# V of four heads with x as the stationary operand, and SiLU gates in pairs of their own

## The chip, the core and the metric

The kernel runs on one core of a Trainium2 chip. The metric is the device time of one execution in microseconds (us). TensorE (PE) multiplies a stationary operand of 128 x 128, which a separate weight load brings in (PEld in the profile), with a streamed (moving) operand of up to 512 columns, into accumulators in PSUM. VectorE (DVE) and ScalarE (ACT) do elementwise work and read PSUM; GpSimd (POOL) and SyncE (SP) here issue transfers. Every product is made from float32 values split in a high and a low part (float32r): high x high + high x low + low x high.

## The reference

One layer over 512 tokens of width 2048, with three token mixers (A: forgetting attention, B: chunked attention, C: stick-breaking attention) of four heads of width 128:

```python
hn = rmsnorm(x, norm_g)
proj = jnp.einsum('bsd,dc->bsc', hn, w_in)
br = proj[..., :QKVG_COLS].reshape(b, s, N_BRANCH, 4, BRANCH_W)      # q, k, v and a gate path for each branch
gates = jax.nn.sigmoid(proj[..., QKVG_COLS + N_HEADS:] + b_gate).reshape(b, s, N_BRANCH, D_MODEL)
...
yc = stick_breaking_attention(to_heads(br[:, :, 2, 0]), to_heads(br[:, :, 2, 1]), to_heads(br[:, :, 2, 2]))
ys = jnp.stack([from_heads(ya), from_heads(yb), from_heads(yc)], axis=2)
ys = ys * jax.nn.silu(br[:, :, :, 3])
up = jnp.einsum('bsnw,nwd->bsnd', ys, w_up)
merged = jnp.sum(gates * up, axis=2)
return x + jnp.einsum('bsd,de->bse', merged, w_out)
```

The change touches V (`br[:, :, n, 2]`), the gate path G (`br[:, :, n, 3]`) and the order of the projection's columns. What is computed stays the same.

## The kernel before, in words

**Layout.** Activations are kept transposed: features on the 128 partitions, the 512 tokens along the free axis. x (times `norm_g`, not yet normalised) lies in SBUF as 16 tiles of 128 features, each as `Parts` with high and low values of two token halves of 256 (`x1`, `x2`, and combinations `t23`, `t4`). A projected column block of 128 (Q, K, V or G of one head, or a 128-wide slice of the merge gates) is one column.

**Pairs.** Two columns are made together by `PairTask` (line 593) with seven products in place of eight (Strassen's scheme in Winograd's form, over two columns, two halves of the 2048 features and two token halves). Each product is a `Pair` unit (line 572) of eight k-steps: the weight block is stationary, x streams. For each k-step there is a 512-wide matmul (`high`, line 667: weight's high part against x's high and low) and a 256-wide one (`low`, line 682: weight's low part against x's high). `stream` (line 1541) goes through the list `units`; a unit may begin with its low step (`low_first`) when the one before ended with its own. Products accumulate onto earlier ones where they can (`onto`), so that the seven use few PSUM banks (`accs`); the other four banks (`atts`) serve attention. `sums` (line 630) makes two of the seven weights on DVE from loaded ones; two are added by POOL's accumulating loads (`add_up`). After a product, `after_of` (line 697) copies or adds it out of PSUM.

**Weights.** SP loads a weight block of 512 KB into one of six `raw` tiles (`NR`). `prep` (line 385) then splits it: ACT copies the high part into `wh` (line 247), DVE subtracts to get `wl` (line 251). There are three buffers of each, and a unit is prepared two units ahead (`LA`).

**Order.** `Flow` plans at build time: generators yield what they wait for and what an engine's next piece costs and when it is due, and the program order of PE, ACT and DVE is written out in the order of that plan. Tiles of 128 x 512 come from a pool of 20 (`t2s`, `NT`). SP's and POOL's queues hold transfers; an instruction there that waits holds up those behind it.

**Units.** The first group (`first_quad`, line 1198, nine units) makes Q, K, V and G of head C0 by direct products, with four banks, while x arrives. Then comes a pair of merge-gate columns; then for each head of C, B and A a pair Q+K, a pair of merge gates, a pair V+G, and a pair of merge gates. Merge-gate columns are normalised and stored to HBM until the up projection. Attention stages (`schedule`, line 1276) are spawned at set units after a head's pairs and mix with the stream on PE.

**V and G of a head.** V comes out with its 128 features on partitions, but the product with the attention weights needs it with tokens on partitions. `v_trans` (line 1087) does four PE transposes into one `att` bank, then four ACT copies (line 1102) and four DVE operations (line 1105) that scale each token by its norm and split into high and low. `silu` (line 1110) normalises G (`by_norm`, line 514), and makes SiLU from it. `av` (line 1133) multiplies V with the attention weights and the result with SiLU.

**After the projections** come the up projection with merge gates (32 units) and the output projection (eight pairs).

Of the kernel before, what the change touches and what calls it, by code (L numbers as in the profile page):

```python
# [15 lines left out]
P = 128  # L16
HP = P // 2
S = 512
# [135 lines left out]
def act_us(n, x=1):  # L154
    return x * (0.075 + 0.00095 * n)
# [7 lines left out]
def hybrid_kernel(  # L163
# [5 lines left out]
    consts: bass.AP,  # L169
    w_one: bass.AP,  # L170
    w_two: bass.AP,
    w_col: bass.AP,
    rel: bass.AP,
    w_up: bass.AP,
# [17 lines left out]
    def nm(s):  # L192
        uid[0] += 1
        return f"{s}_{uid[0]}"
# [16 lines left out]
    def att():  # L211
        return pt.tile([P, S], F32, tag="att", name=nm("att"))
# [4 lines left out]
    def blk(i):  # L217
        return slice(i * P, (i + 1) * P)
# [135 lines left out]
    class Unit:  # L354


        def __init__(self, mms, after=None, shape=(UK, P), srcs=()):
            self.shape, self.mms, self.after, self.srcs = list(shape), mms, after, srcs
            self.ready_hi, self.ready, self.there, self.raw = Event(), Event(), Event(), None
            self.low_first = False  # L360

        def source_there(self):
            return self.there
# [8 lines left out]
        return wp.tile([P] + list(shape), F32, tag="raw", name=nm("raw"), bufs=NR)  # L372

    def load_unit(u):
        if isinstance(u, Pair):
            if u is u.task.units[0]:
                yield from u.task.load()
            return
        for s in u.srcs:
            yield raws, 1  # L380
            t = raw_tile(u.shape)
            u.raw = t
            u.there.t = fetch(t, s, flow.ready, 4 * u.shape[0] * P * P // 1024, nc.scalar if u is units[0] else nc.sync).t

    def prep(u):
        n = u.shape[0] * P
        u.hi = wp.tile([P] + u.shape, F32R, tag="wh", name=nm("wh"), bufs=LA + 1)
        u.lo = wp.tile([P] + u.shape, F32R, tag="wl", name=nm("wl"), bufs=LA + 1)
        yield u.source_there()
        if u is units[0]:  # L390
            for h in range(2):
                yield ACT, act_us(n // 2)
                nc.scalar.activation(u.hi[:, 2 * h:2 * h + 2, :], u.source()[:, 2 * h:2 * h + 2, :], AF.Copy)
                if h == 0:
                    set_(u.ready_hi)
            yield DVE, dve_us(n)
            nc.vector.tensor_sub(u.lo, u.source(), f(u.hi))
            set_(u.ready)
        else:
            yield from split(u.hi, u.lo, u.source(), n, u.ready, hi_ev=u.ready_hi)  # L400
        u.split_done()
# [170 lines left out]
    class Pair(Unit):  # L572


        def __init__(self, task, i):
            super().__init__(task.mms_of(i), task.after_of(i))
            self.task, self.p = task, task.order[i]
            self.single = task.late or task.plain_end and self.p == 4
            self.onto = None if task.late else {6: 1, 7: 6, 4: 7, 3: 5}.get(self.p)

        def source_there(self):
            if self is self.task.units[0]:
# [10 lines left out]
    class PairTask:  # L593
# [9 lines left out]
        def __init__(self, src1, src2, ops, c1_done=None, c2r_done=None, c2_done=None, late=False, rest=None,  # L603
                     x1_first=False, plain_end=False):
            self.plain_end = plain_end
            self.src, self.ops, self.late, self.rest = (*src1, *src2), ops, late, rest
            self.done = {"c1": c1_done, "c2r": c2r_done, "c2": c2_done}
            self.order = (1, 5, 2, 3, 6, 7, 4) if late else (1, 2, 6, 5, 7, 3, 4)
            if x1_first:
                self.order = (1, 5, 6, 2, 7, 3, 4)  # L610
            self.w, self.there, self.ps = {}, {p: Event() for p in range(1, 8)}, {}
            self.ev = {p: Event() for p in range(1, 8)}
            self.r, self.r_ev, self.c2_ev = None, Event(), Event()
            self.units = [Pair(self, i) for i in range(7)]

        def unit(self, p):
# [34 lines left out]
        def mms_of(self, i):  # L651
            p = self.order[i]
            bank = (0, 1, 2, 0, 0, 1, 2)[i] if self.late else {2: 1, 5: 2, 3: 2}.get(p, 0)
            self.bank = getattr(self, "bank", {})
            self.bank[p] = bank

            def go(u):
# [39 lines left out]
        def after_of(self, i):  # L697
# [68 lines left out]
            def go():  # L766
                if i == 0 and self.rest is not None:
                    spawn(self.rest(self), 1.0)
                if self.late:
                    yield from late()  # L770
                    return
                ps, bank = self.ps[p], accs[self.bank[p]]
                if p == 1:
                    yield from new("u")
                    yield a
# [61 lines left out]
            return go  # L837


    gl = {}  # L840
    yd = {}
    f_ev, f2_ev = Event(), Event()
    fd, fd2 = dp.tile([NQ * NH, S], F32, name="fd"), dp.tile([NH, S], F32, name="fd2")

# [41 lines left out]
    class Head:  # L886
# [197 lines left out]
            nc.scalar.activation(z, z, AF.Exp)  # L1084
            set_(self.event("s", i))

        def v_trans(self):
            yield self.event(V)
            for j in range(3):
                yield self.event("hl", j)  # L1090
            yield atts, 1
            yield PE, 0.44
            ps = att()
            for b in range(QB):
                nc.tensor.transpose(ps[:, blk(b)], self.c[V][:, blk(b)], identf)  # L1095
            give(t2s)
            yield t2s, 2
            self.v = h, lo = pair_of("v")
            yield rstd_ev
            yield ACT, 4 * act_us(P)  # L1100
            for b in range(QB):
                nc.scalar.activation(h[:, blk(b)], ps[:, blk(b)], AF.Copy, scale=rcol[:, b:b + 1])
            yield DVE, 4 * dve_us(P)
            for b in range(QB):
                nc.vector.scalar_tensor_tensor(lo[:, blk(b)], ps[:, blk(b)], rcol[:, b:b + 1], f(h[:, blk(b)]),
                                               op0=ALU.mult, op1=ALU.subtract)
            set_(self.event("v"))
            give(atts)
# [48 lines left out]
        def stages(self):  # L1157
# [12 lines left out]
            return g, [(v, self.v_trans), (o - 3, self.silu), (o, self.av)]  # L1170


    def col(n, r, h):
# [13 lines left out]
    def gate_units(late=False, x1_first=False):  # L1187
        n, d = gates.pop(0)

        def keep(i):  # L1190
            def go(c):
# [3 lines left out]
        units.extend(PairTask(gate_col(n, d), gate_col(n, d + 1), ops, keep(0), None, keep(1), late,  # L1195
                              x1_first=x1_first).units)

    def first_quad(head):

        ps, pools = {}, {Q: accs[1], K: accs[2], V: atts, G: atts}  # L1200
        def mms(i):
            def go(u):
# [20 lines left out]
        def take(r):  # L1223
            yield t2s, 1
            c = t2("c")
            if r in (Q, V):
                yield ACT, act_us(S)
                nc.scalar.activation(c, ps[r], AF.Copy)
            else:
                yield DVE, dve_us(S)  # L1230
                nc.vector.tensor_copy(c, ps[r])
            give(pools[r])
            head.c[r] = c
            set_(head.event(r))

# [40 lines left out]
    def schedule(head, a, b):  # L1276
        for (d, g), base in [(g, a) for g in head.stages()[0]] + [(g, b) for g in head.stages()[1]]:
            at(base + d, g, 3.0 if head.last else 5.0)

    def first_head(n, h):  # L1280
        hd = Head(n, h)
        units.extend(first_quad(hd))
        at(OFF["fb"], forget_bias)
        gate_units()
        schedule(hd, OFF["a0"], OFF["b0"])

    def head(n, h, last=False):
# [3 lines left out]
        if not last:  # L1291
            gate_units()
        units.extend(PairTask(col(n, V, h), col(n, G, h), ops, hd.got(V), None, hd.got(G)).units)
        gate_units()
        if last:
            gate_units()
            gate_units(x1_first=True)
        schedule(hd, u0 + 7, u0 + 21)
        return hd

    first_head(C, 0)
    for n, h in [(C, 1), (C, 2), (C, 3)] + [(n, h) for n in (B, A) for h in range(NH)]:
        last_head = head(n, h, (n, h) == (A, NH - 1))


    ys = [None] * 12
# [234 lines left out]
    def stream():  # L1541
        ends_low = False
        for i, u in enumerate(units):
# [7 lines left out]
            if isinstance(u, Pair) and not u.single:  # L1551
# [90 lines left out]
```

## Time and profile before

| | us |
|---|---|
| median of three runs | 1313.18 (1313.05 to 1313.41) |
| the profiled execution | 1313.15 |
| its span, first to last instruction | 1311.4 |
| PE busy in it | 1306.7 |
| DVE busy | 1154.3 |
| ACT busy | 817.8 |
| transfers | 266 MB, mean 203 GB/s |

The granted TensorE clock is 1.0 throughout. A row of the page's groups reads: line of the kernel, engine, operation, tile written <- tiles read, partitions x elements, count | busy us, mean ns of one | idle time of the engine just before, and what ended most of it. A matmul's mean is a latency, as matmuls overlap; its pace is seen from the starts of successive ones. A row of the timeline has start and length in us, engine, line, operation, tiles and count. A row of waits has who waited for whom, the total, the number of waits and the longest, in us. A row of the stretches has its length and then each engine's busy time with its instructions (PE, PEld, DVE, ACT, POOL), the granted clock, the share of the DMA engines and GB/s. A row of transfers has tiles, queue, count, KB of each and median us from issue to landing.

### The profile page before, as it was taken

How to read it: one execution, taken by the hardware profiler on the slowest of the kernel's cores; microseconds unless marked ns; L12 is line 12 of the kernel's file. 1: busy time of each engine (PE TensorE's matmuls, PEld its weight loads, DVE VectorE, ACT ScalarE, POOL GpSimd, SP SyncE). 2: the span in 40 equal slices, each digit the busy share in tenths (PEclk: the TensorE clock that was granted, in tenths of full speed). 3: DMA queues.
4: the chain of work that ended last, by engine and by line, in shares of the span. 5: the costliest groups of instructions: out<-in, count | busy, mean ns of one | idle time of the engine just before them, and what ended most of it. 6: DMA issues, size and time to landing. Idle time of an engine off the chain costs nothing.

```text
span 1311.4 us, 20146 instructions
## 1 busy us (share of the span) xinstructions
PE 1306.7 (100%) x7405; PEld 1143.5 (87%) x7405; DVE 1154.3 (88%) x1723; ACT 817.8 (62%) x1298; POOL 94.8 (7%) x120
## 2 busy tenths in 40 slices
PE   9999999999999999999999999999999999999998
PEld 6888888888888888888888888888888888898887
DVE  8999979788898989988899989899899888897786
ACT  8767657575557665666657665676657655454443
POOL 0010100000010100100100000101000000001000
PEclk9999999999999999999999999999999999999999
DMA  9777676777776777767767777777778855668883
GB/s 344 223 192 190 182 207 170 213 186 194 194 203 190 192 200 187 214 180 194 203 175 221 191 184 201 198 193 187 197 178 277 280 193 168 204 172 254 241 253 95
DMA packets 89794, 266.22 MB, mean 203 GB/s; under 512 B 10704, under 2 KB 12752, under 8 KB 89696
## 3 DMA queue, kind: packets, MB, share of 16 engines
q1 hardware_dynamic: 70400, 203.80, 46.3%
q0 software_dynamic: 15552, 56.63, 25.5%
q10 hardware_dynamic: 3744, 4.52, 1.0%
q8 instruction: 58, 0.95, 0.3%
q14 instruction: 40, 0.33, 0.1%
HBM read 245.21 MB, written 19.70 MB: 202 GB/s over the span
## 4 chain that ended last, share of the span: by engine, by line
PE 99%; DVE 0%; ACT 0%; issue 0%; POOL 0%; ACTq 0%; POOLq 0%
PE acc L266 85%; PE att L266 8%; PE att L1030 1%; PE att L262 1%; PE att L1144 1%; PE att L263 1%; PE att L1145 1%; PE att L261 1%; PE att L1143 1%; PE att L1095 0%; PE att L1245 0%; PE att L1563 0%; PE att L928 0%; DVE m L251 0%; ACT wh L247 0%; DVE wl L251 0%
## 5 line engine op out<-in xcount | busy, mean ns | idle before, releaser
L251 DVE TENSOR_TENSOR wl<-raw,wh 128x1024 fp32r<-128x1024 f32 (+2 forms) x418 | 500.0, 1198 | 103.9 <-ACT wh L247 102.8
L247 ACT ACTIVATE wh<-raw 128x1024 fp32r<-128x1024 f32 (+2 forms) x418 | 434.1, 1039 | 142.2 <-PE acc L266 72.5
L266 PE MATMUL acc<-x,wh 128*128 128x512 f32 x1536 | 394.1, 392 | 0.0
L266 PEld LDWEIGHTS acc<-x,wh 128*128 128x128 f32 x1536 | 281.8, 188 | 56.1 <-issue 2.2
L266 PE MATMUL acc<-t,wh 128*128 128x512 f32 x1104 | 278.9, 393 | 0.0
L266 PEld LDWEIGHTS acc<-t,wh 128*128 128x128 f32 x1104 | 198.5, 189 | 35.3
L266 PEld LDWEIGHTS acc<-x,wl 128*128 128x128 f32 x1504 | 207.8, 190 | 17.1 <-DVE x L450 0.8
L266 PE MATMUL acc<-x,wl 128*128 128x256 f32 (+1 forms) x1504 | 218.9, 285 | 0.0
L266 PE MATMUL acc<-t,wl 128*128 128x256 f32 x1104 | 157.0, 283 | 0.0
L266 PEld LDWEIGHTS acc<-t,wl 128*128 128x128 f32 x1104 | 144.9, 191 | 2.6
L284 POOL DMA_DIRECT2D raw<-in_w_col x92 | 79.5, 864 | 911.1 <-DMA raw<-in_w_col 482.1
L266 PE MATMUL acc<-m,wh 128*128 128x512 f32 (+1 forms) x512 | 109.6, 364 | 0.3 <-DVE m L251 0.3
L266 PEld LDWEIGHTS acc<-m,wh 128*128 128x128 f32 x512 | 86.2, 189 | 13.9 <-DVE m L251 0.5
L797 ACT ACTIVATE u<-acc 128x512 f32<-128x512 f32 x52 | 30.9, 595 | 77.6 <-PE acc L266 75.9
L776 ACT ACTIVATE u<-acc 128x512 f32<-128x512 f32 x53 | 31.8, 599 | 67.8 <-PE acc L266 64.6
L830 ACT ACTIVATE c<-acc 128x256 f32<-128x256 f32 x52 | 19.9, 383 | 83.1 <-PE acc L266 77.6
L642 DVE TENSOR_TENSOR raw<-raw,raw 128x1024 f32<-128x1024 f32 x54 | 65.9, 1221 | 0.5
L636 DVE TENSOR_TENSOR raw<-raw,raw 128x1024 f32<-128x1024 f32 x54 | 65.9, 1220 | 0.3
L266 PE MATMUL att<-y,wh 128*128 128x512 f32 x256 | 65.8, 389 | 0.0
L266 PEld LDWEIGHTS acc<-m,wl 128*128 128x128 f32 x448 | 58.2, 191 | 2.4
L266 PE MATMUL acc<-m,wl 128*128 128x256 f32 x448 | 59.8, 283 | 0.0
L266 PEld LDWEIGHTS att<-y,wh 128*128 128x128 f32 x256 | 48.0, 188 | 10.0
(202 smaller groups left out, 1401.7 us busy)
## 6 DMA issues: line engine op xcount, KB each, us to landing
raw<-in_w_col SPq DMA_DIRECT2D x230, 512.0 KB, 4.3
raw<-in_w_col POOLq DMA_DIRECT2D x92, 512.0 KB, 6.5
raw<-in_w_out SPq DMA_DIRECT2D x40, 512.0 KB, 4.7
gl<-c SPq DMA_DIRECT2D x48, 256.0 KB, 3.0
raw<-in_w_up SPq DMA_DIRECT2D x32, 384.0 KB, 3.2
sg<-gl SPq DMA_DIRECT2D x48, 256.0 KB, 4.3
raw<-in_w_out POOLq DMA_DIRECT2D x16, 512.0 KB, 7.5
xn<-in_xn SPq DMA_DIRECT2D x16, 256.0 KB, 3.3
```

The lines of the kernel that those rows point to most:

```text
L247: nc.scalar.activation(hi, src, AF.Copy)
L251: nc.vector.tensor_sub(lo, src, f(hi))
L261: nc.tensor.matmul(ps, lh, rh, start=start, stop=False, skip_group_check=more)
L262: nc.tensor.matmul(ps, lh, rl, start=False, stop=False, skip_group_check=more)
L263: nc.tensor.matmul(ps, ll, rh, start=False, stop=stop, skip_group_check=more)
L266: nc.tensor.matmul(ps, w, x, start=start, stop=stop, skip_group_check=more)
L284: nc.gpsimd.dma_start(to, src, accum_op=ALU.add)
L636: nc.vector.tensor_add(w[1], w[1], w[5])
L642: nc.vector.tensor_add(w[2], w[2], w[1])
L776: nc.scalar.activation(self.u, ps, AF.Copy)
L797: nc.scalar.activation(self.s, ps, AF.Copy)
L830: nc.scalar.activation(c, ps[:, RH], AF.Copy, scale=-1.0)
```

## The change

- **V.** A `ValueTask` makes V of a branch's four heads (512 columns) at once by the same seven products: x's block of 128 features by 128 tokens is stationary, the weights stream (high and low parts of 256 columns side by side). It has 14 units: each product's eight k-steps are cut in two halves of four, and each half serves two blocks of tokens (`subs`, two `PairTask`s that only supply the steps after the products). The result has tokens on partitions; ACT scales it by each token's norm, SP stores it to HBM, and `value` reads a head's part back and splits it. The transposes are gone. The second block of tokens uses one `att` bank and banks of `accs[0]`.
- **G.** Gates are made in pairs of two heads; the second head's is normalised, stored to HBM and read back in `silu` (`far`, `gd`). In the first group G of head C1 takes the place of V.
- **Order.** `HEADS` lists what follows each head's Q+K pair: s a pair of gates G, g a pair of merge gates, v the next branch's V task. C's V task comes right after the first group. The offset `b0` goes from 20 to 23.
- **Weights.** High and low parts share one tile (`u.w`), in all units. The weights of V's product 7 are loaded, for each half, into two tiles of the `t2s` pool in place of a `raw` tile.

```diff
     def prep(u):
-        n = u.shape[0] * P
-        u.hi = wp.tile([P] + u.shape, F32R, tag="wh", name=nm("wh"), bufs=LA + 1)
-        u.lo = wp.tile([P] + u.shape, F32R, tag="wl", name=nm("wl"), bufs=LA + 1)
+        n = u.shape[0] * u.shape[1]
+        u.w = wp.tile([P, 2] + u.shape, F32R, tag="w", name=nm("w"), bufs=LA + 1)
+        u.hi, u.lo = u.w[:, 0], u.w[:, 1]
...
+        elif isinstance(u.source(), list):
+            h = u.shape[0] // 2
+            for i, t in enumerate(u.source()):
+                ks, evs = slice(i * h, (i + 1) * h), (u.ready, u.ready_hi) if i else (None, None)
+                yield from split(u.hi[:, ks], u.lo[:, ks], t, n // 2, evs[0], hi_ev=evs[1])
...
+    class ValueTask:
+        def __init__(self, n, ops):
...
+            self.units = [VUnit(self, p, kh) for p in (1, 2, 6, 5, 7, 3, 4) for kh in range(2)]
+            self.dram = [[dp.tile([P, S], F32, name=nm("vd")) for _ in range(2)] for _ in range(2)]
...
+            self.subs = [PairTask((None, None), (None, None), ops, self.keep(0, s), None, self.keep(1, s))
+                         for s in range(2)]
+            self.subs[1].pools, self.subs[1].tile = [atts, accs[0], accs[0]], lambda b: acc() if b else att()
+        def keep(self, g, s):
+            def go(c):
+                yield rstd_ev
+                for i, h in enumerate((LH, RH)):
+                    yield ACT, act_us(HS)
+                    nc.scalar.activation(c[:, h], c[:, h], AF.Copy, scale=rcol[:, 2 * i + s:2 * i + s + 1])
+                nc.sync.dma_start(self.dram[g][s], c)
...
+        def load(self):
+            def src(i, kh):
+                return w_v[self.n, i // 2, i % 2, kh]
+            for p, kh in ((1, 0), (1, 1), (5, 0), (2, 0), (2, 1), (5, 1), (7, 0), (7, 1), (4, 0), (4, 1)):
+                srcs = {5: (2, 3), 1: (0,), 2: (1,), 7: (0, 2), 4: (3,)}[p]
+                if p == 7:
+                    yield t2s, 2
+                    ts = [t2("raw").rearrange("p (j c) -> p j c", j=2) for _ in range(2)]
+                    self.w[p, kh] = ts
+                else:
+                    yield raws, 1
+                    t = self.w[p, kh] = raw_tile((UK // 2, 2 * P))
+                    ts = [t]
...
+        def sums(self):
+            n = dve_us(UK * P)
+            for a, b, p, q in ((1, 5, 6, 5), (2, 6, 3, 6)):
+                for kh in range(2):
...
+                    yield DVE, n, flow.ready + (1.0 if p == 6 else 5.0)
+                    nc.vector.tensor_add(self.w[a, kh], self.w[a, kh], self.w[b, kh])
...
+        def mms(self, u):
...
+            def high(s):
+                yield from begin(s)
+                yield u.ready
+                ps = self.subs[s].ps[p]
+                for j in range(UK // 2):
...
+                    yield PE, mm_us(S)
+                    mm(two(ps), r[:, 0, blocks[s]], u.w[:, :, j, :], u.opens and j == 0, False, True)
+            def low(s):
...
+                    yield PE, mm_us(HS)
+                    mm(ps[:, LH], r[:, 1, blocks[s]], u.hi[:, j, :], False, False, True)
+            h, l = high, low
+            steps = ((l, 0), (l, 1), (h, 0), (h, 1)) if u.low_first else ((h, 0), (h, 1), (l, 0), (l, 1))
...
-        def v_trans(self):
-            yield self.event(V)
+        def value(self):
+            g, d = self.h // 2, self.h % 2
+            task = values[self.n]
+            for s in range(2):
+                yield task.kept[g][s]
             for j in range(3):
                 yield self.event("hl", j)
...
-            for b in range(QB):
-                nc.tensor.transpose(ps[:, blk(b)], self.c[V][:, blk(b)], identf)
+            yield t2s, 1
+            t = t2("vr")
+            to = t.rearrange("p (i s d) -> p i s d", i=2, s=2)
+            for s in range(2):
+                ev = fetch(to[:, :, s, :], task.dram[g][s].rearrange("p (i h d) -> p i h d", i=2, h=2)[:, :, d, :],
+                           flow.now, 128)
+            yield ev
+            yield t2s, 2
+            self.v = pair_of("v")
+            yield from split(*self.v, t, S, self.event("v"))
             give(t2s)
...
         def silu(self):
-            yield self.event(G)
-            g = self.c[G]
-            yield from by_norm(g)
+            if (self.n, self.h) in gd:
+                d, ev = gd[self.n, self.h]
+                yield ev
+                yield t2s, 1
+                g = t2("g")
+                yield fetch(g, d, flow.now, 256)
+            else:
+                yield self.event(G)
+                g = self.c[G]
+                yield from by_norm(g)
...
+    def far(n, h):
+        d, ev = gd[n, h] = dp.tile([P, S], F32, name=nm("gd")), Event()
+        def go(c):
+            yield from by_norm(c)
+            nc.sync.dma_start(d, c)
...
-                u.low_first = ends_low and u.onto is not None and low_there
+                u.low_first = ends_low and not u.opens and (low_there or isinstance(u, VUnit))
...
-OFF = dict(cs=3, ct=12, s=11, t=17, v=1, av=8, s1=8, t1=13, v1=0, av1=3, fb=24, a0=11, b0=20)
+ONTO = {6: 1, 7: 6, 4: 7, 3: 5}
+HEADS = [(C, 1, "gg"), (C, 2, "sgg"), (C, 3, "gv"), (B, 0, "sgg"), (B, 1, "ggg"), (B, 2, "sgg"), (B, 3, "gv"),
+         (A, 0, "sgg"), (A, 1, "gg"), (A, 2, "sgg"), (A, 3, "gggg")]
+OFF = dict(cs=3, ct=12, s=11, t=17, v=1, av=8, s1=8, t1=13, v1=0, av1=3, fb=24, a0=11, b0=23)
...
+    vals = w[:, :nq].reshape(2, 2, UK // 2, P, NB, 4, 2, 2 * P)[:, :, :, :, :, V]
...
-    cols = [C * 4 * NH + r * NH for r in range(4)]
+    cols = [C * 4 * NH + c for c in (Q * NH, K * NH, G * NH + 1, G * NH)]
```

More of the change, by code (lines that the diff above doesn't have):

```diff
@@ L171, in hybrid_kernel @@
     w_two: bass.AP,
+    w_v: bass.AP,
     w_col: bass.AP,
@@ L578, in __init__ @@
             self.single = task.late or task.plain_end and self.p == 4
-            self.onto = None if task.late else {6: 1, 7: 6, 4: 7, 3: 5}.get(self.p)
+            self.onto = None if task.late else ONTO.get(self.p)
+            self.turns, self.opens = not self.single, self.onto is None
         def source_there(self):
@@ L837, in after_of, with __init__, source_there, source @@
             return go
+    class VUnit(Unit):
+        def __init__(self, task, p, kh):
+            super().__init__(task.mms, None, (UK // 2, 2 * P))
+            self.task, self.p, self.kh, self.onto = task, p, kh, ONTO.get(p)
+            self.turns, self.opens = True, self.onto is None and kh == 0
+        def source_there(self):
+            if self is self.task.units[0]:
+                spawn(self.task.sums(), 1.5)
+            return self.task.there[self.p, self.kh]
+        def source(self):
+            return self.task.w[self.p, self.kh]
+        def split_done(self):
+            if self.p in (3, 4):
+                give(raws)
+            elif self.p == 7:
+                give(t2s, 2)
@@ L1283, in first_head, with head @@
         at(OFF["fb"], forget_bias)
+        value_units(n)
         gate_units()
         schedule(hd, OFF["a0"], OFF["b0"])
-    def head(n, h, last=False):
+    def head(n, h, more, last=False):
         hd = Head(n, h, last)
@@ L1290, in head @@
         units.extend(PairTask(col(n, Q, h), col(n, K, h), ops, hd.got(Q), None, hd.got(K)).units)
[L1291 to L1297, printed above, removed]
+        for i, what in enumerate(more):
+            if what == "v":
+                value_units(n - 1)
+            elif what == "s":
+                units.extend(PairTask(col(n, G, h), col(n, G, h + 1), ops, hd.got(G), None, far(n, h + 1)).units)
+            else:
+                gate_units(x1_first=last and i == len(more) - 1)
         schedule(hd, u0 + 7, u0 + 21)
@@ L1301, in hybrid_kernel @@
     first_head(C, 0)
-    for n, h in [(C, 1), (C, 2), (C, 3)] + [(n, h) for n in (B, A) for h in range(NH)]:
-        last_head = head(n, h, (n, h) == (A, NH - 1))
+    for n, h, more in HEADS:
+        last_head = head(n, h, more, (n, h) == (A, NH - 1))
     ys = [None] * 12
```

95 lines of the change are left out of this document (74 added, 21 removed).

## The prediction

> **What bounds the kernel now.** I read the page first, then who TensorE (PE) waited for, then stretches of its timeline.
>
> ```profile
> span 1311.4 us, 20146 instructions
> PE 1306.7 (100%) x7405; PEld 1143.5 (87%) x7405; DVE 1154.3 (88%) x1723; ACT 817.8 (62%) x1298; POOL 94.8 (7%) x120
> PE att L1563 <- POOL nhepsc L309: 1.1, 1, 1.1
> PE acc L266 <- DVE m L251: 0.3, 1, 0.3
> ```
>
> PE works through the whole span; its waits come to 1.4 us, 1.1 of them before its first matmul. A busy PE alone proves little, as its matmuls are pipelined, so I take its pace from the starts of successive groups in an undisturbed stretch:
>
> ```profile
> 423.64 1.11 PE L266 MATMUL acc<-x,wl 128*128 128x256 f32 x8
> 424.59 1.12 PE L266 MATMUL acc<-t,wl 128*128 128x256 f32 x8
> 425.55 2.00 PE L266 MATMUL acc<-t,wh 128*128 128x512 f32 x8
> 427.39 1.98 PE L266 MATMUL acc<-x,wh 128*128 128x512 f32 x8
> 429.20 1.12 PE L266 MATMUL acc<-x,wl 128*128 128x256 f32 x8
> ```
>
> Eight 512-wide matmuls take 1.81 to 1.84 us (427.39 - 425.55), eight 256-wide ones 0.95 to 0.96, a unit 2.78. They follow with no gap, so whatever leaves PE's list is gained, provided that no new wait opens.
>
> **The change, part by part.**
>
> *The transposes of V go.* Four in each of 12 heads:
>
> ```profile
> L1095 PE MATMUL att<-identf,c 128*128 128x128 f32 x48 | 7.2, 272 | 0.0
> 754.86 1.52 PE L266 MATMUL acc<-x,wh 128*128 128x512 f32 x6
> 756.22 0.60 PE L1095 MATMUL att<-identf,c 128*128 128x128 f32 x4
> 756.57 0.70 PE L266 MATMUL acc<-x,wh 128*128 128x512 f32 x2
> 757.12 1.11 PE L266 MATMUL acc<-x,wl 128*128 128x256 f32 x8
> 405.19 0.85 PE L266 MATMUL acc<-x,wh 128*128 128x512 f32 x3
> 405.88 0.60 PE L1095 MATMUL att<-identf,c 128*128 128x128 f32 x4
> 406.31 0.38 PE L1030 MATMUL att<-identf,p 128*128 128x128 f32 x2
> 406.45 1.40 PE L266 MATMUL acc<-x,wh 128*128 128x512 f32 x5
> 407.68 1.12 PE L266 MATMUL acc<-x,wl 128*128 128x256 f32 x8
> ```
>
> The mean of 272 ns is a pipelined latency. What four of them hold up is read from the starts. From 754.86 to 757.12 eight 512-wide matmuls and four transposes take 2.26 us; the eight alone take 1.82, so the four cost 0.44. In the second stretch eight matmuls and six transposes take 2.49, so six cost 0.67 and four 0.44 again. Over 12 heads: 12 x 0.44 = 5.3 us; with 1.81 or 1.84 for the eight the bounds are 5.0 and 5.4.
>
> [...] The starts show that successive ones overlap. [...]
>
> *V's products exchange their operands.* A V task replaces two pairs (four heads' V), and has 14 units in place of 2 x 7. Each half unit's four k-steps times two token blocks make eight 512-wide and eight 256-wide matmuls: a pair unit's list. Elements streamed, matmuls and weight loads are equal. G's pairs move from V+G to G+G, and the number of G and V columns in all is the same (head C1's G takes V's place in the first group of four). What is new is that the streamed operand is two runs of 256 (hi and lo of a weight). The first group already streams x.hi as two separate runs:
>
> ```profile
> 12.80 0.62 PE L266 MATMUL att<-x,wh 128*128 128x512 f32 x2
> 13.71 0.61 PE L266 MATMUL att<-x,wh 128*128 128x512 f32 x2
> ```
>
> Four start in 0.91 us (two into acc lie between), 0.228 each, the same pace as eight in 1.81 to 1.84. So I take nothing for the exchange; the spread of 0.03 us per eight over 42 V units bounds it by 1.3 us either way.
>
> *The 512-wide step now needs the weight's low half.* Before, a unit begins with its high half, and VectorE (DVE) may finish the low one while PE works. In V the streamed block holds both, so PE waits for DVE's subtraction too. The tightest place that I found:
>
> ```profile
> 373.49 1.22 DVE L251 TENSOR_TENSOR wl<-raw,wh 128x1024 fp32r<-128x1024 f32 x1
> 374.62 2.00 PE L266 MATMUL acc<-t,wh 128*128 128x512 f32 x8
> 376.46 1.12 PE L266 MATMUL acc<-t,wl 128*128 128x256 f32 x8
> ```
>
> The low half is ready at 374.71, 0.09 after its unit starts and 1.75 before it is used. In V that 0.09 would stop PE, and with it the attention matmuls queued behind. Such spots lie where a pair starts, as it wants its sum of two weights at once; in V the first sum is wanted only by the fifth unit. DVE's load in the stretches where V tasks come:
>
> ```profile
> 50.00:100.00 50.00, 50.00 (x282) 43.79 (x281) 46.80 (x67) 35.96 (x63) 4.29 (x5) 1.00 0.72 177
> 300.00:350.00 50.00, 50.00 (x292) 44.14 (x291) 41.70 (x55) 26.44 (x39) 4.38 (x6) 1.00 0.74 196
> 650.00:700.00 50.00, 50.00 (x292) 44.19 (x291) 41.66 (x57) 34.25 (x52) 4.34 (x5) 1.00 0.70 198
> ```
>
> The third number of work is DVE's: 94% in the first, where the combinations of x are also made, 83% in the other two. Bounds: 0 if every low half is early, 42 x 0.09 = 3.8 us if each is as late as the row. I take 0.5 us, all in the first task: five or six units at 0.09. If that cover failed outright there, the slower rival below is the price.
>
> *VectorE and ScalarE (ACT).*
>
> ```profile
> L1105 DVE SCALAR_TENSOR_TENSOR vl<-att,small_n,vh 128x128 fp32r<-128x128 f32 x48 | 13.5, 345 | 0.5 <-ACT vh L1102 0.5
> L251 DVE TENSOR_TENSOR qkl<-rs,qkh 128x512 fp32r<-128x512 f32 x16 | 11.0, 685 | 0.0
> L251 DVE TENSOR_TENSOR wl<-raw,wh 128x1024 fp32r<-128x1024 f32 x385 | 468.8, 1220 | 100.6 <-ACT wh L247 99.6
> L1102 ACT ACTIVATE vh<-att,small_n 128x128 fp32r<-128x128 f32 x48 | 13.7, 371 | 2.6 <-PE att L1095 2.3
> L247 ACT ACTIVATE qkh<-rs 128x512 fp32r<-128x512 f32 x16 | 10.0, 627 | 3.6 <-DVE rs L936 3.6
> L830 ACT ACTIVATE c<-acc 128x256 f32<-128x256 f32 x52 | 19.9, 383 | 83.1 <-PE acc L266 77.6
> L247 ACT ACTIVATE wh<-raw 128x1024 fp32r<-128x1024 f32 x385 | 406.4, 1057 | 109.6 <-PE acc L266 71.5 <-issue 18.2 <-DVE raw L636 7.7
> ```
>
> DVE loses 48 x 0.345 = 16.6 us and gains 12 whole-tile splits x 0.685 = 8.2. The seventh product's weights, split as two tiles of 512, add 6 x (2 x 0.685 - 1.220) = 0.9: net -7.5. ACT loses 48 x 0.371 = 17.8 and gains 12 x 0.627 = 7.5, 24 scalings of 256 columns at about 0.383 = 9.2, and 6 x (2 x 0.627 - 1.057) = 1.2: about 0. G's normings are as many as before. None of it is on PE's path: 0, hidden behind PE.
>
> *High and low halves become one tile,* in every unit. ACT's split into a new one then waits until both halves of the unit that had the buffer are used, where it now waits for the high half's matmuls alone:
>
> ```profile
> ACT wh L247 <- PE acc L266: 72.5, 67, 3.6
> ```
>
> Where a unit ends on its low matmuls this puts the split up to 0.96 us later (eight 256-wide), and ACT's work behind it. A split is made two units (5.56 us) ahead and takes 1.06 on ACT and 1.22 on DVE, so 2.3 us of room remain after a loss of 0.96: 0 on PE's path. Without that room each such unit would lose part of the 0.96; it adds to the chance of the slower rival.
>
> *Transfers.* V goes to HBM (12 x 256 KB) and comes back (24 x 128 KB); six G's go and come (256 KB each way): 9.4 MB on 266. SP gets 18 stores, 30 reads and six more weight loads (12 for a V task against 10 for two pairs); POOL's adding loads are six more.
>
> ```profile
> raw<-in_w_col SPq DMA_DIRECT2D x230, 512.0 KB, 4.3
> raw<-in_w_col POOLq DMA_DIRECT2D x92, 512.0 KB, 6.5
> gl<-c SPq DMA_DIRECT2D x48, 256.0 KB, 3.0
> sg<-gl SPq DMA_DIRECT2D x48, 256.0 KB, 4.3
> SPq L278 <- DVE wl L251: 680.6, 251, 10.2
> ```
>
> A round trip is 3.0 + 4.3 = 7.3 us. The nearest use is head C0: its V is complete in the eleventh and twelfth of the task's 14 units, the read is due 3 units later (8.3 us), when the store has long landed, and the product with V 7 units after the read. A store on SP waits for ACT, and the weight loads behind it wait too; but SP already waits up to 10.2 us for room, and the row of ACT's splits of wh names PE, issue and DVE, no transfer, as what ended its idle time. Cost 0; below, a rival prices it.
>
> **The sum**: 1313.15 us, this execution's own time (span 1311.4 and 1.75 around it; the median of the runs is 1313.18), - 5.3 + 0.5 = **1308.4 us**. Its own range, with 5.0 to 5.4 for the transposes, 0 to 3.8 for the low halves and 1.3 either way for the pace (both extremes at once unlikely): 1307 to 1311.
>
> **Rivals.**
>
> *Low halves late in the first V task (slower).* From 50 to 100 us DVE is 94% busy with the combinations of x, whose due times come earlier than the splits'. If in each of the 14 units one operation of a 512-wide tile (0.685 us) gets ahead of the subtraction, PE stops 14 x 0.685 = 9.6 us: 1313.15 - 5.3 + 9.6 = 1317.5. It decides from 5.3 / 14 = 0.38 us a unit. For: a unit has 2.78 us, the buffers allow preparing only two ahead, and the joint tile takes 0.96 of that. Against: 7.5 us of work leave DVE, and V's sums come later than a pair's.
>
> *A load comes late once.* A V task takes all six raw tiles before its third product, and its seventh product's sums are two adding loads of half the size each. If one falls a unit behind, PE loses 2.78: 1308.4 + 2.8 = 1311.2, no difference that can be told. Against: a source and its adding load land within 4.3 + 6.5 = 10.8 us, about four units, and the queues show longer waits than that borne today. [...]
>
> *The transposes are worth their full latency*: 48 x 0.272 = 13.1 us, 1300.1 us. For: the row of 272. Against: the two stretches above.
>
> **How the numbers follow.** The forecast 0.66; a late load or a slower pace, ending within 1310.5 to 1313.5, 0.16; low halves or loads late enough to end slower 0.15; the full latency 0.03. About 0.2% (2.6 us) is what a measurement can tell from no change, so faster ends below 1310.6. Nearly all of the forecast and the last lie there, with a part of the second: 0.75; same 0.11; slower 0.14. The range 1306.9 to 1313.5 leaves out the slower cases and the last.
>
> **What would show it.** PE should have 48 matmuls less, no new row among its waits above a few tenths, and V's groups of eight at 1.81 to 1.84 and 0.95 us. A wait of PE for DVE's wl in the first 100 us would show the slower rival; one for a transfer, the second. It is wrong if V's groups start further apart, or if PE has idle time elsewhere, such as at scores that lack one of the four att banks, since a V task holds one.

## The result and the profile after

| | before | after |
|---|---|---|
| median | 1313.42 us (1313.05 to 1313.71, 6 runs) | 1320.85 us (1320.19 to 1322.49, 6 runs) |
| ratio | | 1.0059, 95% interval 1.0046 to 1.0072 |
| span of the profiled execution | 1311.4 us | 1319.3 us |
| mean granted clock | 1.000 | 0.997 |

The change makes the kernel 7.4 us slower, where 5 us less were forecast. The page of the changed kernel gives the span, the engines' busy times, and the shares of the chain that ended last:

```profile
span 1319.3 us, 20167 instructions
PE 1305.7 (99%) x7357; PEld 1141.1 (86%) x7357; DVE 1149.1 (87%) x1693; ACT 824.0 (62%) x1292; POOL 100.3 (8%) x126
PE 92%; DMA 3%; DVE 3%; issue 1%; ACT 1%; POOL 0%; DVEq 0%; ACTq 0%; POOLq 0%
```

PE has 48 matmuls less, as it should, but it no longer works through the span, and the chain now holds 3% of transfers. Its row of waits shows what is new:

```profile
PE acc L267 <- DVE w L252: 8.7, 3, 4.3
PE att L1741 <- POOL nhepsc L310: 1.1, 1, 1.1
PE acc L267 <- DVE m L252: 0.3, 1, 0.3
```

The first row is new: three waits for a weight's low half. The other two were there before. The three lie one in each V task. The timeline of PE has them at 61, 321 and 660 us (in brackets the idle time and what ended it):

```profile
61.20 2.11 PE L267 MATMUL acc<-w,x 128*128 128x512 f32 x8 [0.98 <-DVE w L252]
...
321.45 1.19 PE L267 MATMUL acc<-w,t 128*128 128x512 f32 x4 [3.41 <-DVE w L252]
...
659.61 1.39 PE L267 MATMUL acc<-w,t 128*128 128x512 f32 x4 [4.33 <-DVE w L252]
```

A wait for DVE need not mean that DVE had too much to do. Who DVE waited for, the kernel before in the first row and the changed kernel in the other two:

```profile
DVE wl L251 <- ACT wh L247: 102.8, 93, 2.1
...
DVE w L252 <- ACT w L248: 101.6, 103, 2.2
DVE raw L937 <- DMA raw<-in_w_v: 13.9, 4, 6.0
```

The waits for ACT are as before. The last row has no counterpart: in the kernel before DVE waits for one load in all, at the start (1.7 us), and here its sums of two weights (line 937) stand and wait for loads of V's weights. All engines around the second wait:

```profile
304.61 4.43 POOL L285 DMA_DIRECT2D raw<-in_w_v  x5 [8.55 <-DMA raw<-in_w_v]
...
318.57 1.22 DVE L937 TENSOR_TENSOR raw<-raw,raw 128x1024 f32<-128x1024 f32 x1 [5.99 <-DMA raw<-in_w_v]
319.71 0.55 DVE L1236 TENSOR_TENSOR z<-z,lk 128x384 f32<-128x384 f32 x1
320.18 1.22 DVE L252 TENSOR_TENSOR w<-raw,w 128x1024 fp32r<-128x1024 f32 x1
```

DVE is idle for 6 us, then makes the sum, a small operation, and the subtraction that PE has waited for. The sum is that of product 6's second half, (6,1); the subtraction belongs to the first half, (6,0), whose sum was done. ACT's copy for it ended at 314.06, so it was ready 6 us before it started, and stood behind an instruction that was not. In the third task, the chain of waits leads from the sum back to the load (columns: start, length, what):

```profile
638.75 9.68 DMA raw<-in_w_v
...
648.47 0.49 issue
648.96 8.21 DMA raw<-in_w_v
...
657.19 0.04 DVE raw L937
657.23 1.11 issue
658.33 1.23 DVE w L252
...
659.61 1.39 PE acc L267 x4
```

A load of 9.7 us and an adding load of 8.2: 17.9 us, with 0.5 between them. They belong to (5,1), the last half weight to get one of the six `raw` tiles. Reading the order of the transfers on SP's queue out of the changed kernel's instructions, in the second task:

```
tile       what           size
raw_3106   (2,1)          128x1024
raw_3144   product 7      128x512
raw_3145   product 7      128x512
raw_3150   product 7      128x512
raw_3151   product 7      128x512
raw_3141   (5,1)          128x1024
```

The source of `load` asks for (5,1) before product 7. The order on SP's queue is not written out by hand, and the scheduler put the four part loads of product 7 ahead, which use tiles of their own and are wanted later. POOL's adding loads came in the same order (four parts, then 3141). So the load that is wanted first is fifth, on both queues. In the third task (5,1) is behind all four parts as well. In the first it stands ahead of them, so that the wait at 61 us must have another reason.

What happened after the two long waits shows in the stretches of the changed kernel (the granted clock is the third number from the end):

```profile
317.66:321.45 3.79, 0.39 (x2) 0.00 (x0) 2.88 (x4) 1.15 (x2) 0.00 (x0) 1.00 0.02 4
321.45:325.90 4.45, 4.45 (x17) 3.90 (x18) 4.45 (x6) 1.27 (x2) 0.00 (x0) 0.62 0.00 0
659.61:664.10 4.49, 4.49 (x17) 3.87 (x18) 4.49 (x8) 1.21 (x2) 0.00 (x0) 0.62 0.00 2
```

Once PE is back, its granted clock is 0.62 over 4.5 us; cut finer, it is 0.50 from 322.53 to 325.94 and from 660.45 to 663.86, called the half clock below. At a clock of 1.00 that work would take 4.5 x 0.62 = 2.8 us by estimate, so 1.7 us go at each place, 3.4 in all.

### The profile page after: what moved, and what is told of

It reads as the page before. It is cut to its first block, busy times and chain, and to the rows that moved or that the text cites. A ratio compares the mean times of both kernels' runs of the same rounds, so it can differ in the third digit from the quotient of the medians.

```text
span 1319.3 us, 20167 instructions
## 1 busy us (share of the span) xinstructions
PE 1305.7 (99%) x7357; PEld 1141.1 (86%) x7357; DVE 1149.1 (87%) x1693; ACT 824.0 (62%) x1292; POOL 100.3 (8%) x126
## 4 chain that ended last, share of the span: by engine, by line
PE 92%; DMA 3%; DVE 3%; issue 1%; ACT 1%; POOL 0%; DVEq 0%; ACTq 0%; POOLq 0%
PE acc L267 78%; PE att L267 9%; DMA raw<-in_w_v 3%; DVE w L252 1%; PE att L1185 1%; PE att L1302 1%; PE att L1303 1%; PE att L263 1%; PE att L264 1%; PE att L1301 1%; PE att L262 1%; DVE m L252 0%; PE att L1741 0%; ACT w L248 0%; PE att L1083 0%
## 5 line engine op out<-in xcount | busy, mean ns | idle before, releaser
L252 DVE TENSOR_TENSOR w<-raw,w 128x1024 fp32r<-128x1024 f32 (+2 forms) x424 | 501.3, 1184 | 102.8 <-ACT w L248 101.6
L248 ACT ACTIVATE w<-raw 128x1024 fp32r<-128x1024 f32 (+2 forms) x424 | 435.4, 1028 | 231.6 <-PE acc L267 116.6
L267 PE MATMUL acc<-x,w 128*128 128x512 f32 (+1 forms) x2656 | 502.7, 339 | 0.0
L267 PEld LDWEIGHTS acc<-x,w 128*128 128x128 f32 x2656 | 425.4, 189 | 65.4 <-issue 3.0
L267 PE MATMUL acc<-t,w 128*128 128x512 f32 (+1 forms) x1920 | 360.8, 338 | 0.0
L267 PEld LDWEIGHTS acc<-t,w 128*128 128x128 f32 x1920 | 291.1, 190 | 32.2
L267 PE MATMUL acc<-m,w 128*128 128x256 f32 (+1 forms) x960 | 157.3, 326 | 0.3 <-DVE m L252 0.3
L267 PEld LDWEIGHTS acc<-m,w 128*128 128x128 f32 x960 | 141.3, 190 | 16.3 <-DVE m L252 0.5
L267 PE MATMUL att<-y,w 128*128 128x512 f32 x384 | 89.6, 389 | 0.0
L267 PEld LDWEIGHTS att<-y,w 128*128 128x128 f32 x384 | 72.1, 188 | 14.9
```

Source lines behind the costliest of these rows:

```text
L248: nc.scalar.activation(hi, src, AF.Copy)
L252: nc.vector.tensor_sub(lo, src, f(hi))
L267: nc.tensor.matmul(ps, w, x, start=start, stop=stop, skip_group_check=more)
```

## The experiments

My theory after the comparison: the order on SP's queue makes (5,1) late, its sum blocks DVE, and PE's idle time brings the half clock with it. Rivals: DVE is overloaded by the combinations of x; the exchange of operands or the joint tile costs time; the half clock comes from somewhere else. Each kernel was timed beside the kernel before on the same chip.

### The order on SP's queue (pin)

```diff
-    def fetch(to, src, ready, kb, queue=nc.sync):
+    def fetch(to, src, ready, kb, queue=nc.sync, pin=False):
         i = queue.dma_start(to, src)
+        if pin:
+            tc.keep_in_program_order(i)
...
-                            ev = fetch(t, part, flow.ready, kb)
+                            ev = fetch(t, part, flow.ready, kb, pin=p == 7)
```

> Only the order of SP's queue changes: in a V task the second half of product 5's weights is issued before the four part loads of product 7 (and so POOL's adding loads follow in that order). Theory, the order: the 10.7 us that this half's adding load takes comes from the four part loads and adds ahead of it; both long waits of PE (3.6 us at 318, 4.5 us at 655) vanish, the low clock after them too (3.3 us), 1309.5 us. Rival, the room: the last of six raw tiles comes free too late (about 300 and 639 us) in any order; PE still waits over 2 us at both places, 1316 or more.

Measured: 1310.5 us (1310.12 to 1312.4), ratio to before 0.9979 (0.997 to 0.9989), 10.3 less than the change and 1.0 above the theory's figure. `raw_3141` now stands ahead of `raw_3144` on SP's queue, and its adding load ahead of theirs on POOL's. The stretch in which the changed kernel's PE stood at 318 us:

```profile
317.66:321.45 3.79, 3.79 (x23) 3.27 (x22) 3.79 (x6) 1.06 (x1) 0.00 (x0) 1.00 0.01 3
```

And the waits of PE and of DVE in pin:

```profile
PE acc L267 <- DVE w L252: 1.5, 1, 1.5
...
PE acc L267 <- ACT w L396: 0.5, 1, 0.5
...
DVE raw L939 <- DMA raw<-in_w_v: 2.9, 3, 1.7
```

In this trace the two long waits and the half clock are gone. No other line was changed, and the same transfers are made, so it was their order and neither their number nor the room in the `raw` tiles. What is left is the wait of the first task, at 60 us. The trace is of a run of 1310.18 us with a mean granted clock of 1.000; three of the ten runs took 1312.4 us with 0.998 or 0.999, so some executions of pin still lose clock, and no trace shows where.

### Parts of the change alone (before_no_transposes, before_joint_tile)

In the kernel before, without V's transposes: V's splits read the untransposed product.

```diff
-            yield atts, 1
-            yield PE, 0.44
-            ps = att()
-            for b in range(QB):
-                nc.tensor.transpose(ps[:, blk(b)], self.c[V][:, blk(b)], identf)
-            give(t2s)
+            ps = self.c[V]
```

> The kernel before, without V's 48 transposes: the four copies of a head read V as it came (so V is not transposed). What the transposes are worth: by the starts of matmuls 5.3 us, 1308.1; by their latency of 272 ns 13.1 us, 1300.3; nothing if PE's time is taken by something else, 1313.4.

Measured: 1308.27 us (1308.01 to 1308.56) against 1313.69: -5.4, ratio 0.9959 (0.9946 to 0.9971). The transposes are worth what the starts in the timeline gave, not their latency.

In the kernel before, with the joint tile for high and low parts:

```diff
-        u.hi = wp.tile([P] + u.shape, F32R, tag="wh", name=nm("wh"), bufs=LA + 1)
-        u.lo = wp.tile([P] + u.shape, F32R, tag="wl", name=nm("wl"), bufs=LA + 1)
+        u.w = wp.tile([P, 2] + u.shape, F32R, tag="w", name=nm("w"), bufs=LA + 1)
+        u.hi, u.lo = u.w[:, 0], u.w[:, 1]
```

> The kernel before with the high and low part of each weight in one tile, as in the change, and nothing else. Theory: ACT's splits start up to 0.96 us later, PE does not see it, 1313.5. Rival: PE loses part of that at the tight pairs; over 1316.

Measured: 1313.63 us (1313.42 to 1314.47) against 1313.79, ratio 0.9998 (0.999 to 1.0007). No cost that can be measured.

### The sum moved, the load left (later)

```diff
                     yield self.there[a, kh]
+                    if p == 6 and kh == 1:
+                        yield self.unit(6, 0).ready
```

> SP's order as in the change; in DVE's order the sum for product 6's second half now stands behind the subtraction of product 6's first half. Theory, the queue: what PE waited for was ready, and stood on DVE behind a sum that waited for a late load; now PE waits one unit later and less, about 1.7 us at 318 and 3.0 at 655 with little loss of clock, about 1315. Rival: product 6's first half itself is late; waits and time as in the change, 1320.9.

Measured: 1319.33 us (1318.87 to 1320.38), 1.5 less than the change, where about 1315 was expected. The wait at 318 us is gone, so (6,0) indeed stood behind the other half's sum. But the load stays late, and (6,1) itself now waits for it in the third task (1.5 and 1.2 us, with a clock of 0.51 from 660.70 to 666.80 behind them). The edit moves the first task's sums as well. The wait there grew from 0.98 to 2.24 us, and another of 1.26 opened at 75; the timeline of PE has the first:

```profile
62.52 2.07 PE L267 MATMUL acc<-w,x 128*128 128x512 f32 x4 [2.24 <-DVE w L252]
```

The stretch that begins there has a clock of 0.51:

```profile
62.50:66.00 3.50, 3.48 (x8) 2.79 (x9) 3.50 (x7) 0.91 (x2) 0.00 (x0) 0.51 0.64 155
```

So moving the sum unblocks one place and starves others; the lateness is in the load.

### The first task's wait (due60, pin_first, pin_one, pin_load)

At 60 us, pin still loses 1.5 us. The combinations of x come 5 us later (`due60`, on the changed kernel):

```diff
-DUE = 45.0, 55.0
+DUE = 45.0, 60.0
```

> The due time of the later combinations of x goes from 55 to 60 us in the order written for DVE. Theory: the 1.1 us that PE waits at 60 us comes from combinations ahead of the weight's low half; it goes, 1319.7 us, and the two later waits stay. Rival: copies out of PSUM and normings ahead of it make the wait; it stays, 1320.9.

Measured: 1320.09 us (1318.98 to 1322.53); the wait at 61 us falls from 0.98 to 0.52 in the profiled run, and another of 0.70 opens at 72. It doesn't support DVE's load as the cause, nor does it settle it.

In pin, DVE's first sum waits for its adding load again (timeline of DVE):

```profile
55.47 1.23 DVE L939 TENSOR_TENSOR raw<-raw,raw 128x1024 f32<-128x1024 f32 x1 [1.73 <-DMA raw<-in_w_v]
...
60.69 1.23 DVE L252 TENSOR_TENSOR w<-raw,w 128x1024 fp32r<-128x1024 f32 x1
```

Pin with both sums of that task placed 4 us later (`pin_first`), or with the first of them alone 2.5 us later (`pin_one`):

```diff
+                    if p == 6 and self.n == C:
+                        yield Event(flow.ready + 4.0)
```

```diff
+                    if p == 6 and kh == 0 and self.n == C:
+                        yield Event(flow.ready + 2.5)
```

> The run pin, and in the first V task the two sums for product 6 are placed 4 us later in the order for DVE. Theory: the wait of 1.6 us left at 60 us comes from DVE standing 1.7 us in its first sum, whose adding load lands late, with the subtractions behind it; it goes, 1309.0. Rival: DVE has too much to do there (combinations of x, copies, normings); the wait stays, 1310.5.

> The run pin, and in the first V task only the first of product 6's two sums is placed 2.5 us later in the order for DVE (pin_first had moved both by 4 us and more, and opened waits at 69 and 71 us). Theory: PE's wait at 60 us comes from DVE standing in that sum until its adding load lands; it falls from 1.6 us to below 0.4 and no other opens, 1309.0. Rival: DVE has too much to do there; the wait moves to a later unit, 1310.5 or more.

Measured: pin_first 1314.14 us (1313.37 to 1315.02), slower than pin by 3.6: the wait at 60 us is gone, but the second sum was now too late itself, PE waited 0.9 us at 70 and 2.0 at 73, and the clock fell, as two stretches of pin_first show:

```profile
71.30:73.40 2.10, 0.22 (x2) 0.01 (x1) 2.10 (x3) 0.00 (x0) 0.00 (x0) 0.87 0.69 250
73.40:79.50 6.10, 6.03 (x16) 4.91 (x17) 2.05 (x4) 2.70 (x7) 0.86 (x1) 0.50 0.70 252
```

pin_one 1308.65 us (1308.64 to 1309.47), ratio 0.9962 (0.9949 to 0.9976), the best version, and faster than the kernel before. Its page:

```profile
span 1307.2 us, 20171 instructions
PE 1302.2 (100%) x7357; PEld 1138.6 (87%) x7357; DVE 1148.3 (88%) x1693; ACT 823.8 (63%) x1292; POOL 100.3 (8%) x126
```

All waits of its PE, and the two operations of its DVE that answer to pin's two above:

```profile
PE att L1745 <- POOL nhepsc L312: 1.1, 1, 1.1
PE acc L267 <- DVE m L252: 0.3, 1, 0.3
```

```profile
56.99 1.21 DVE L941 TENSOR_TENSOR raw<-raw,raw 128x1024 f32<-128x1024 f32 x1
...
59.40 1.22 DVE L252 TENSOR_TENSOR w<-raw,w 128x1024 fp32r<-128x1024 f32 x1
```

PE's waits are those of before. DVE does other work first, starts the sum 1.5 us later without idle time, and the low half is begun at 59.40 instead of 60.69. With as many instructions on DVE as in pin (1693), the wait is gone: it was the place of one sum, and with it of the work around it, not the amount of work.

Another way to bring the adding load earlier is to load product 5 first (`pin_load`, on pin):

```diff
-            for p, kh in ((1, 0), (1, 1), (5, 0), (2, 0), (2, 1), (5, 1), (7, 0), (7, 1), (4, 0), (4, 1)):
+            for p, kh in ((5, 0), (1, 0), (1, 1), (2, 0), (5, 1), (2, 1), (7, 0), (7, 1), (4, 0), (4, 1)):
```

> The run pin, with product 5's first half loaded first of all in each V task and its second half ahead of product 2's second half. Theory: the adding load of the first sum starts some 2 us earlier, DVE does not stand in it, the wait at 60 us falls below 0.5, 1309.2. Rival: now product 1, the first to be used, comes late, and PE waits at the start of the task; 1310.5 or more.

Measured: 1314.57 us (1313.09 to 1315.96). PE waits 0.4, 0.7 and 1.8 us, one in each task. The time is the rival's, but not its mechanism: PE does not wait at the start of a task for product 1, but two units later or more, for low halves of product 2. In the second and third task DVE stands 1.7 and 1.9 us in a sum that waits for its load, with that subtraction behind it.

### The half clock (fill, fill2)

In the tasks of B and A, 14 more matmuls of 512 columns, whose result nobody reads, in product 6's second half (`fill`, with `kh == 1`) or its first (`fill2`, with `kh == 0`):

```diff
+            if p == 6 and kh == 1 and self.n != C:
+                yield atts, 1
+                spare = att()
+                for _ in range(14):
+                    nc.tensor.matmul(two(spare), ones_r, x1[0].both(0)[0], start=True, stop=True)
+                give(atts)
```

> 14 matmuls of 512 columns that nobody reads are put where PE waits in the second and third V task (3.2 us of work in each wait of 3.6 and 4.5 us). Theory, the clock: the wait itself is as long as before, but PE is not idle for long, the granted clock stays at 1 and the 3.3 us that matmuls lose right after both waits are saved: 1317.6 us. Rival: the matmuls after the waits are slow for another reason (their operands come late one by one); the time stays 1320.9.

> As before with the 14 extra matmuls, but now directly ahead of the product 6 first half, where PE's waits of 3.6 and 4.5 us lie (the earlier place was one unit behind them). Theory, the clock: the waits end when they did, PE idles 0.4 and 1.3 us instead, the granted clock stays at 1, the matmuls after the waits keep 227 ns and the time falls by 3.3 us to 1317.5. Rival: those matmuls are slow for another reason, 1320.9.

fill: 1327.11 us (1324.88 to 1327.92). The matmuls came one unit behind the waits, and so filled nothing: 28 x 0.227 = 6.4 us of work more, and PE's three waits are 8.6 us as before. By the sum used for fill2 below, with one stretch of half clock left (0.72 and 0.85 over 660 to 664 and 664 to 668, 1.7 us), the span should be 1323.9; it is 1324.8, and 0.9 stays open. The run shows one thing: the first of the long waits, now 2.44 us, had a clock of 1.00 behind it. The timeline of PE, and the stretch behind that wait:

```profile
322.00 1.21 PE L267 MATMUL acc<-w,t 128*128 128x512 f32 x4 [2.44 <-DVE w L252]
```

```profile
322.00:326.00 4.00, 4.00 (x21) 3.46 (x22) 4.00 (x6) 2.16 (x3) 0.00 (x0) 1.00 0.00 0
```

fill2: 1319.51 us (1319.27 to 1321.71), between the theory's 1317.5 and the rival's 1320.9; here they lie in the waits. The waits for w fall to 3.2 us and the clock stays up: its mean is 1.000 in all four runs, against 0.996 to 0.998 in the six of the change. Two stretches, and PE's wait:

```profile
317.50:321.50 4.00, 4.00 (x19) 3.24 (x18) 3.22 (x4) 1.49 (x3) 0.00 (x0) 1.00 0.01 2
321.50:326.00 4.50, 4.50 (x29) 3.99 (x28) 4.50 (x7) 1.61 (x2) 0.00 (x0) 1.00 0.00 0
```

```profile
PE acc L267 <- DVE w L252: 3.2, 3, 1.7
```

The theory's figure counted the added work as all hidden in the waits, which it was not. By the spans: 1319.3 + 6.4 of work - 5.5 of waits (8.7 - 3.2) + 0.7 (a wait for ACT at the start) - 3.4 of half clock = 1317.5; its span is 1317.6. Without the 3.4 this sum gives 1320.9 and doesn't close: the half clock cost what the granted clock gives, and here it went with the idle time. The load was as late as ever (DVE still stands 13.0 us in the sums), and PE had other work meanwhile.

## Why the prediction was wrong

**What held.** The kernel is bound by PE, and PE's own work fell as forecast. The transposes gave 5.4 us alone (forecast 5.3). V's groups follow at the old pace, as the timeline of the changed kernel shows:

```profile
306.75 1.07 PE L267 MATMUL acc<-w,x 128*128 128x512 f32 x4
307.66 1.07 PE L267 MATMUL att<-w,x 128*128 128x512 f32 x4
308.56 0.64 PE L267 MATMUL acc<-w,x 128*128 128x256 f32 x4
309.04 0.64 PE L267 MATMUL att<-w,x 128*128 128x256 f32 x4
```

Eight of 512 take 308.56 - 306.75 = 1.81 us; four of 256 take 0.48. The joint tile cost nothing that can be measured (ratio 0.9998). With the order of the loads and the place of one sum put right (pin_one) the kernel takes 1308.65 us against the 1308.4 forecast, so the sum was right for all that PE does, and what failed lies in one step.

**The step that failed** is "Transfers ... Cost 0". In its place the runs show 8.7 us of waits of PE and 3.4 us of half clock behind them. The step looked at single round trips, at V's stores, and at waits borne today. In its rival it took "a source and its adding load land within 4.3 + 6.5 = 10.8 us" from medians of the pairs' loads. Three things went wrong there.
- It counted six more weight loads for the V tasks and asked how long each takes, but not *where in the queue* it is issued. The part loads need `t2s` tiles and not `raw` ones; the scheduler placed them ahead of the load that waited for the sixth `raw` tile, in the second and third task.
- Load and adding load then took 17.9 us in the third task, not 10.8. V's loads among the rows of transfers in the changed kernel (the last number is the median from issue to landing, against 4.3 and 6.5 for the pairs' loads before); the first row is all whole loads, the late (5,1) among them, the second product 7's parts, the third the adding loads of product 5. The median of the whole loads is as before, so a median would not have shown the late one:

```profile
raw<-in_w_v SPq DMA_DIRECT2D x24, 512.0 KB, 4.4
...
raw<-in_w_v SPq DMA_DIRECT2D x12, 256.0 KB, 9.4
raw<-in_w_v POOLq DMA_DIRECT2D x6, 512.0 KB, 8.4
```

- It read it as room that "the row of ACT's splits of wh names PE, issue and DVE, no transfer". That is ACT's row, and the transfers held up DVE. DVE executed in order here, as the subtraction of (6,0) shows, whose input was there at 314.06 and which began at 320.18, behind the sum. It stood 13.9 us in sums that waited for transfers, and held subtractions whose inputs were there.

**The rivals.** "A load comes late once" has the mechanism, but one unit, once: 2.8 us, "no difference that can be told". In truth PE waits in each V task, the longest in the second and third, where (5,1) is late. The chances gave "low halves or loads late enough to end slower" 0.15, but a price for such a time was worked out for the low halves alone. "Low halves late" named the wait that PE shows, and its sign; its cause, DVE's 94% load in the first task, was not it. The long waits lie where DVE had idle time, and pin removes them with DVE's work unchanged. That PE was granted only 0.62 of its clock for 4.5 us after each of the two long waits was in no case.

**The account.** In the session of pin_one, whose PE has the waits of before, the medians are 1313.77 before and 1308.65 with it: 5.1 us less, of which the transposes alone gave 5.4. The 0.3 left over is too small to be split among the low halves (0.5 in the forecast), the exchange and the joint tile. By the spans of single executions, pin_one's 1307.2 + 8.7 of waits + 3.4 of half clock = 1319.3, the changed kernel's span.

**Sizes off the path.** DVE's busy time fell by 5.2 us (1154.3 to 1149.1) and not 7.5; ACT's rose by 6.2 (817.8 to 824.0) and not by 0. Neither sets the time.

**Open.** Why the scheduler places the four part loads ahead was not tried. Its order on SP's queue was seen, and that the time follows it. Why ACT has more to do was not looked into.

## What to carry to other kernels

When a change adds loads that draw on another pool of buffers, look at the order in which all loads reach the queue, and at which one waits for its buffer: with the issue order of four loads as its only edit, pin took 10.3 us off the changed kernel. When an engine that is not the bottleneck executes in order, a waiting instruction in front of ready work counts like lost time of the engine that needs that work, so ask for each sum or copy of the planned order what it waits for and who stands behind it. And look at the granted clock behind each stall of PE: here 7.7 us of idle time in two places cost 3.4 more through the clock. Two short stalls close together did the same: in later, waits of 1.5 and 1.2 us between 656 and 661 came with a clock of 0.51 from 660.70 to 666.80. In fill, a wait of 2.44 us had 1.00 behind it.

## What the runs showed of the hardware

Half clock after idle time was expected by no step. After 3.41 and 4.33 us without work, PE was granted 0.62 over the next 4.5 us. Cut finer, the clock of the changed kernel is 0.50 from 322.53 to 325.94 and from 660.45 to 663.86, and 1.00 in the stretches around both:

```profile
319.11:322.53 3.42, 1.07 (x5) 0.90 (x6) 3.42 (x5) 2.23 (x3) 0.00 (x0) 1.00 0.01 2
322.53:325.94 3.41, 3.41 (x14) 3.04 (x13) 3.41 (x6) 0.19 (x1) 0.00 (x0) 0.50 0.00 0
325.94:329.36 3.42, 3.42 (x20) 2.98 (x20) 3.42 (x5) 2.45 (x4) 0.00 (x0) 1.00 0.49 155
657.03:660.45 3.42, 0.84 (x4) 0.71 (x5) 3.26 (x4) 1.64 (x2) 0.00 (x0) 1.00 0.01 2
660.45:663.86 3.41, 3.41 (x13) 2.93 (x12) 3.41 (x7) 0.37 (x1) 0.00 (x0) 0.50 0.00 0
663.86:667.27 3.41, 3.41 (x21) 3.03 (x21) 3.41 (x4) 1.87 (x3) 0.00 (x0) 1.00 0.35 102
```

Two waits of like length were not followed by the same clock. In later, behind the 2.24 us of idle time at 62, the clock was 0.51 from 62.50 to 66.00; in fill, behind the 2.44 us at 322, it was 1.00 from 322.00 to 326.00. The stretches just ahead, later in the first row and fill in the second:

```profile
59.80:62.50 2.70, 0.48 (x3) 0.06 (x1) 2.70 (x6) 2.39 (x6) 0.00 (x0) 1.00 0.99 177
319.00:322.00 3.00, 0.56 (x3) 0.14 (x1) 2.88 (x4) 1.15 (x2) 0.00 (x0) 1.00 0.01 3
```

PE was busy for 0.48 of 2.70 us in the one and 0.56 of 3.00 in the other. So the length of a wait alone does not tell what clock comes behind it. What decides that clock was not shown: no run set out to move a wait, or to change its length, with all else as it was.
